# Stick-breaking attention: one scan and one product for both heads of a pair

## The chip, the cores and the metric

The kernel runs on one core of a Trainium2 chip. The metric is the device time of one execution in microseconds, the median of several runs. Times inside an execution come from the hardware profiler's trace of one execution. The engines are TensorE (PE in the profile, its weight loads PEld), VectorE (DVE), ScalarE (ACT), GpSimd (POOL) and SyncE (SP), on whose queue most DMAs are issued.

## The reference

The model is a trunk of two residual layers over 512 tokens of width 1024. Layer 0 mixes tokens with eight stick-breaking attention heads beside a state space model, layer 1 with sparse attention; each mixer is followed by an MLP, and a layer norm stands behind each of the four parts. The change is in the stick-breaking heads:

```python
z = jnp.einsum('bqhd,bshd->bhqs', q_b, k).astype(jnp.float32) * scale
causal = (spos[None, :] < tpos[:, None])[None, None]
log_beta = jax.nn.log_sigmoid(z)
log_1mb = jnp.where(causal, jax.nn.log_sigmoid(-z), 0.0)
csum = jnp.cumsum(log_1mb, axis=-1)
log_w = log_beta + csum[..., -1:] - csum
w = jnp.where(causal, jnp.exp(log_w), 0.0).astype(v.dtype)
return jnp.einsum('bhqs,bshd->bqhd', w, v)
```

The weight of key s is sigmoid(z_s) times the product of sigmoid(-z) over all later keys. There are 8 heads of 64 columns, and queries go in blocks of 128.

## The kernel before, in words

The kernel is one program for one core. It is written with a framework that tracks the tiles, puts a wait wherever two instructions share one, and plans the order of all engines' instructions when the program is built, by a model of their times; so an instruction need not stand in its queue where the source has it. Each engine then executes its own queue in order. A tile that is allocated with a tag takes turns among that tag's buffers, and a new user waits until the old one's readers are done. `tc.issue_after(x)` puts instructions behind x on the same engine.

`mixer_sb_ssm` (L666) is layer 0's mixer. It projects the input, runs the state space model in four groups, and projects q and k in four pairs of heads (`projections`, L763). Then a pool "att" is opened (L747), the norm's parameters are loaded (`gb`, L749, with the two DMAs of L168 and L169), and the attention of pairs 0, 1 and 2 follows, the gate of the state space model (`glu`, L776), pair 3, and the output projection in two halves (L760 and L761). The second half ends in the first layer norm, which reads `gb` at L185 and L189. The tag "gb" has one buffer; before `gb` it holds the phases `e` of the state space model (L514), which L616, L617, L627 and L628 read.

`stack_qk` (L880) splits a pair's q and k into a high and a low part (ScalarE at L889, GpSimd at L890) and moves them by DMA into `qst` and `kst`. `attention` (L901) does one pair: for each of four query blocks (`qb`), with nk = 128, 256, 384 or 512 keys, TensorE makes the logits of both heads in two PSUM banks (L914) and adds the causal mask (L918). Then, for each head in turn: ScalarE makes e = sigmoid(-z/8) (L922) and bt = sigmoid(z/8) (L923); VectorE scans e from the last key to the first with state = e * state + 0, starting from 1, into w (L925), reading the addend from one column of zeros with step 0; and it multiplies w by bt (L926). The e that the scan reads is shifted by one key, and GpSimd writes a 1 behind the last (L921). e has three buffers and bt two, each for one head; w has two, each for both heads. TensorE transposes the weights (`transpose_weights`, L934, L942), ScalarE copies them out of PSUM (L943), and TensorE multiplies by the values (L949). The marks of L931 place the first half of the output projection: its eight blocks stand behind nothing, nothing, nothing, and then the weighted values of query blocks 0, 0, 1, 1 and 2 of the last pair.

Of the kernel before, what the change touches and what calls it, by code (L numbers as in the profile page):

```python
# [8 lines left out]
F32 = mybir.dt.float32  # L9
F32R = mybir.dt.float32r  # L10
AF = mybir.ActivationFunctionType
ALU = mybir.AluOpType
# [3 lines left out]
P = 128  # L16
S = 512
D = 1024
KT = D // P
NB = S // P  # L20
# [15 lines left out]
class Trunk:  # L36
# [629 lines left out]
    def mixer_sb_ssm(self, w_in, w_out, w_glu, g, b):  # L666
        nc, a, tc = self.nc, self.a, self.tc
        act, vec, pool = nc.scalar, nc.vector, nc.gpsimd
        with tc.tile_pool(name="ps0", bufs=2, space=PSUM) as self.psb, \
# [76 lines left out]
            self.load_x()  # L746
            with tc.tile_pool(name="att", bufs=2, reuse_waits="tile") as ap:  # L747
                self.hlp = ap
                gb = self.ln_params(g, b)  # L749
                chi, clo = self.xhi, self.xlo  # L750
                rows = lambda kk, c0: self.w_rows(w_out, kk * 256, c0)
                att = lambda pr: self.attention(pr, self.stack_qk(qks[pr], ap), ap, v, msk_r)
                att(0)
                att(1)
                att(2)
                with tc.issue_after(self.last_move.ins):
                    self.fill_x()
                self.glu(w_glu, bgl, uTs, [t[:, i, :] for t in qks[:2] for i in range(2)], chi, clo)
                att(3)
                self.out_proj(chi, clo, rows, range(4, 8), True, None)  # L760
                self.out_proj(chi, clo, rows, range(4), False, gb)  # L761

    def projections(self, w_in, v, qks):  # L763

# [136 lines left out]
    def attention(self, pr, qk, ap, v, msk_r):  # L901

        nc = self.nc
        act, vec = nc.scalar, nc.vector
        qst, kst = qk
        self.kept = True
        cs = slice(pr * P, (pr + 1) * P)
        for qb in range(NB):
            nk = (qb + 1) * P
            qs = slice(qb * P, (qb + 1) * P)  # L910
            zs = [self.abank([P, 512], "psz") for _ in range(2)]
            for h in range(2):
                for part in range(2):
                    nc.tensor.matmul(zs[h][:, :nk], qst[:, h, qs], kst[:, h, part, :nk], start=part == 0, stop=False)  # L914
            w = ap.tile([P, 2, S], F32, tag="aw", name=self.nm("aw"))
            zero = self.zero.to_broadcast([P, nk])
            for h in range(2):
                nc.tensor.matmul(zs[h][:, nk - P:nk], self.ident_r, msk_r, start=False, stop=True)  # L918
                e = ap.tile([P, S + 1], F32, tag="ae", bufs=3, name=self.nm("ae"))
                bt = ap.tile([P, S], F32, tag="ab", bufs=2, name=self.nm("ab"))  # L920
                nc.gpsimd.memset(e[:, nk:nk + 1], 1.0)  # L921
                act.activation(e[:, :nk], zs[h][:, :nk], AF.Sigmoid, scale=-0.125)  # L922
                act.activation(bt[:, :nk], zs[h][:, :nk], AF.Sigmoid, scale=0.125)  # L923
                wv = w[:, h, :nk]
                vec.tensor_tensor_scan(wv[:, ::-1], e[:, 1:nk + 1][:, ::-1], zero, 1.0, ALU.mult, ALU.add)  # L925
                vec.tensor_tensor(wv, wv, bt[:, :nk], ALU.mult)  # L926
            wt = ap.tile([P, NB, 2, P], F32, tag="wt", name=self.nm("wt"))
            self.transpose_weights(w, wt, qb, nc.scalar.copy)
            if qb == 0:
                po = self.abank([P, S], "pso", True)  # L930
            self.marks[qb] = self.weighted_values(po[:, qs], wt, v, (cs.start, cs.start + 64), qb)  # L931
        self.split(self.xhi[:, pr, :], self.xlo[:, pr, :], po)
# [275 lines left out]
```

## Time and profile before

| | us |
|---|---|
| median of 3 runs | 1164.22 |
| the three runs | 1163.82, 1164.22, 1166.73 |
| the profiled execution | 1163.17 |
| its span, first to last instruction | 1161.4 |

In the profile, a line such as L925 is a line of the kernel, and `aw<-ae,two` names the tile that is written and those that are read: `ae` is e, `ab` is bt, `aw` is w, `wt` the transposed weights, `psz` the logits, `pst` the transposes in PSUM, `pso` the weighted values. In a timeline, a row gives the start, how long it took, the engine, the line, and how many instructions were merged into the row (the first one's shape is printed); in brackets stands how long the engine had been idle before it and who ended that. A matmul's recorded time holds its pipeline's latency too, so that rows of TensorE overlap.

### The profile page before, as it was taken

Reading aid. Unit: us, or ns where it says so; the run is one execution under the profiler, and the core shown is the slowest. Engines: PE = TensorE matmul, PEld = TensorE weight load, DVE = VectorE, ACT = ScalarE, POOL = GpSimd, SP = SyncE. Lnnn points to the kernel's source line nnn. Section 1 sums busy time; section 2 is a strip of 40 time slices with the busy share of each in tenths; the row PEclk is TensorE's granted clock in tenths of the full one; section 3 lists DMA queues with packets and bytes.
Section 4 is the critical chain, followed back from the end, with each engine's and each line's share of the span. In section 5 each row is a group of like instructions: output and inputs, shape, how many; then the busy total and the mean of one; then the engine's idle time right before and its main releaser. Section 6 shows DMA issues by size and latency. Waiting matters only on the chain.

```text
span 1161.4 us, 15563 instructions
## 1 busy us (share of the span) xinstructions
PE 1111.9 (96%) x5860; PEld 926.4 (80%) x5860; DVE 840.6 (72%) x1255; ACT 532.6 (46%) x832; POOL 172.2 (15%) x201
## 2 busy tenths in 40 slices
PE   7989999999999999999999979997999999999997
PEld 6878877779888888888898867775988888888886
DVE  7996598694667875965568998557548678587736
ACT  5534386424544444554135446552445445445520
POOL 1043230320000000000121655325000000000001
PEclk9998999999999999999999989998999999999999
DMA  7526683651243252333046860008304415315101
GB/s 246 143 62 157 189 223 96 194 168 39 61 145 101 62 159 73 97 112 87 1 120 158 216 189 1 2 9 264 109 19 127 131 33 152 120 38 162 37 1 73
DMA packets 147307, 126.99 MB, mean 109 GB/s; under 512 B 24353, under 2 KB 115297, under 8 KB 147233
## 3 DMA queue, kind: packets, MB, share of 16 engines
q1 hardware_dynamic: 145552, 123.59, 36.9%
q10 hardware_dynamic: 1680, 2.41, 0.6%
q8 instruction: 46, 0.75, 0.3%
q14 instruction: 29, 0.23, 0.1%
HBM read 105.80 MB, written 5.37 MB: 96 GB/s over the span
## 4 chain that ended last, share of the span: by engine, by line
PE 85%; DVE 6%; DMA 4%; issue 2%; ACT 2%; SPq 1%; POOL 0%; POOLq 0%; DVEq 0%; ACTq 0%
PE psa L131 12%; PE psa L133 12%; PE psa L132 12%; PE psb L311 7%; PE psb L313 7%; PE psb L312 7%; PE pso L949 3%; PE pst L942 3%; PE psb L382 3%; PE psb L381 3%; PE psb L380 3%; PE psl L1142 2%; PE psb L841 2%; PE psb L842 2%; PE psb L843 2%
## 5 line engine op out<-in xcount | busy, mean ns | idle before, releaser
L133 PE MATMUL psa<-xhi,wlo 128*128 128x512 f32 (+1 forms) x720 | 267.0, 371 | 0.0
L132 PE MATMUL psa<-xlo,whi 128*128 128x512 f32 (+1 forms) x720 | 266.5, 371 | 0.0
L131 PE MATMUL psa<-xhi,whi 128*128 128x512 f32 (+1 forms) x720 | 265.6, 371 | 0.2 <-ACT xhi L202 0.2
L104 ACT CAST whi<-raw 128x1024 fp32r<-128x1024 f32 (+1 forms) x129 | 133.6, 1046 | 204.6 <-PE psa L132 126.4
L105 DVE TENSOR_TENSOR wlo<-raw,whi 128x1024 fp32r<-128x1024 f32 (+1 forms) x102 | 128.2, 1260 | 86.9 <-ACT whi L104 85.8
L132 PEld LDWEIGHTS psa<-xlo,whi 128*128 128x128 f32 x720 | 135.7, 188 | 23.3 <-DVE xlo L203 0.4
L133 PEld LDWEIGHTS psa<-xhi,wlo 128*128 128x128 f32 x720 | 135.7, 188 | 23.2
L131 PEld LDWEIGHTS psa<-xhi,whi 128*128 128x128 f32 x720 | 135.0, 188 | 23.1 <-ACT xhi L202 0.5
L299 DVE TENSOR_TENSOR wlo<-b,whi 128x1024 fp32r<-128x1024 f32 x84 | 102.6, 1222 | 42.9 <-ACT whi L298 42.8
L311 PE MATMUL psb<-whi,whi 128*128 128x512 f32 x336 | 130.7, 389 | 0.0
L312 PE MATMUL psb<-wlo,whi 128*128 128x512 f32 x336 | 130.7, 389 | 0.0
L313 PE MATMUL psb<-whi,wlo 128*128 128x512 f32 x336 | 129.7, 389 | 0.0
L298 ACT CAST whi<-b 128x1024 fp32r<-128x1024 f32 x84 | 88.3, 1051 | 41.9 <-PE psb L313 30.2
L105 POOL TENSOR_TENSOR wlo<-raw,whi 128x1024 fp32r<-128x1024 f32 x27 | 69.7, 2591 | 135.6 <-ACT whi L104 134.5
L184 POOL TENSOR_TENSOR rs<-rs,two 128x1 f32<-128x1 f32 x16 | 22.4, 1402 | 424.2 <-DVE rs L183 424.2
L313 PEld LDWEIGHTS psb<-whi,wlo 128*128 128x128 f32 x336 | 63.1, 188 | 13.2
L312 PEld LDWEIGHTS psb<-wlo,whi 128*128 128x128 f32 x336 | 63.1, 188 | 13.1
L311 PEld LDWEIGHTS psb<-whi,whi 128*128 128x128 f32 x336 | 63.1, 188 | 13.0
L293 DVE TENSOR_TENSOR b<-b,b 128x1024 f32<-128x1024 f32 x48 | 60.3, 1262 | 12.3 <-DMA b<-in_w_dram 11.8
L298 ACT CAST whi<-h 128x1024 fp32r<-128x1024 f32 x36 | 38.0, 1054 | 54.0 <-PE psb L312 34.0
L299 DVE TENSOR_TENSOR wlo<-h,whi 128x1024 fp32r<-128x1024 f32 x36 | 44.0, 1222 | 14.2 <-ACT whi L298 13.5
L841 PE MATMUL psb<-whi,xhi 128*128 128x512 f32 x128 | 51.6, 411 | 0.8 <-DVE rs L183 0.6
(263 smaller groups left out, 1967.5 us busy)
## 6 DMA issues: line engine op xcount, KB each, us to landing
raw<-in_w_dram SPq DMA_DIRECT2D x80, 512.0 KB, 4.1
b<-in_w_dram SPq DMA_DIRECT2D x48, 512.0 KB, 4.6
raw<-in_w_in_dram SPq DMA_DIRECT2D x29, 512.0 KB, 4.4
raw<-in_w_out_dram SPq DMA_DIRECT2D x16, 512.0 KB, 4.6
qst<-hl SPq DMA_DIRECT2D x48, 128.0 KB, 3.5
kst<-hl SPq DMA_DIRECT2D x24, 256.0 KB, 4.4
gb<-in_ln_g_dram SPq DMA_DIRECT2D x4, 512.0 KB, 4.0
gb<-in_ln_b_dram SPq DMA_DIRECT2D x4, 512.0 KB, 5.2
```

Source lines behind the costliest of these rows:

```text
L104: nc.scalar.copy(hi[:, c], raw[:, c])
L105: (eng or nc.vector).tensor_tensor(lo[:, c], raw[:, c], hi[:, c].bitcast(F32), ALU.subtract)
L131: mm(ps, lhi, rhi, start=start, stop=False)
L132: mm(ps, lhi, rlo, start=False, stop=False)
L133: mm(ps, llo, rhi, start=False, stop=stop)
L293: vec.tensor_tensor(o, p, q, op)
L298: act.copy(hi, src)
L299: vec.tensor_tensor(lo, src, hi.bitcast(F32), ALU.subtract)
L311: mm(ps, lh, bhi[:, k, :], start=i + k == 0, stop=False)
L312: mm(ps, lh, blo[:, k, :], start=False, stop=False)
L313: mm(ps, ll, bhi[:, k, :], start=False, stop=i + k == 2)
L841: nc.tensor.matmul(ps, chi[:, k, tok], whi, start=i == 0, stop=False)
```

## The change

For each block of queries, e and bt become one tile each for both heads, with the two heads' columns one behind the other; there are two sets of them, for odd and for even blocks, each with one buffer. e has one column more than 2 x nk, and GpSimd writes zeros at columns nk and 2 nk, where a head begins when it is read backward. One scan over 2 x nk columns takes e as its factor and a row of zeros and ones as its addend: at the first column of each head the factor is 0 and the addend 1, so the state becomes 1, and everywhere else the addend is 0. Then one multiply does both heads. ScalarE no longer computes e for key 0, which the scan does not read.

The rows of zeros and ones for the four block lengths are overlapping windows of one strip of 1792 columns, filled by GpSimd before the attention. The strip lies in the tag "gb", where the norm's parameters lay; those are now loaded after the attention, at the call of the second half of the output projection. The tile w is read as one row of 2 x nk columns.

```diff
--- before.py
+++ after.py
@@ -746,7 +746,16 @@
             self.load_x()
             with tc.tile_pool(name="att", bufs=2, reuse_waits="tile") as ap:
                 self.hlp = ap
-                gb = self.ln_params(g, b)
+
+                ones = self.cp.tile([P, 2, D], F32, tag="gb", bufs=1, name="ones").rearrange("p r d -> p (r d)")
+                pool.memset(ones[:, 0:1792], 0.0)
+                self.ones, at = [None] * NB, 511
+                pool.memset(ones[:, at:at + 1], 1.0)
+                for qb in (3, 2, 1, 0):
+                    nk = (qb + 1) * P
+                    self.ones[qb] = ones[:, at - nk + 1:at + nk + 1]
+                    at += nk
+                    pool.memset(ones[:, at:at + 1], 1.0)
                 chi, clo = self.xhi, self.xlo
                 rows = lambda kk, c0: self.w_rows(w_out, kk * 256, c0)
                 att = lambda pr: self.attention(pr, self.stack_qk(qks[pr], ap), ap, v, msk_r)
@@ -758,7 +767,7 @@
                 self.glu(w_glu, bgl, uTs, [t[:, i, :] for t in qks[:2] for i in range(2)], chi, clo)
                 att(3)
                 self.out_proj(chi, clo, rows, range(4, 8), True, None)
-                self.out_proj(chi, clo, rows, range(4), False, gb)
+                self.out_proj(chi, clo, rows, range(4), False, self.ln_params(g, b))
 
     def projections(self, w_in, v, qks):
 
@@ -913,17 +922,20 @@
                 for part in range(2):
                     nc.tensor.matmul(zs[h][:, :nk], qst[:, h, qs], kst[:, h, part, :nk], start=part == 0, stop=False)
             w = ap.tile([P, 2, S], F32, tag="aw", name=self.nm("aw"))
-            zero = self.zero.to_broadcast([P, nk])
+
+            tag, n = (f"{qb % 2}", S if qb % 2 else 384)
+            e = ap.tile([P, 2 * n + 1], F32, tag="ae" + tag, bufs=1, name=self.nm("ae"))[:, :2 * nk + 1]
+            bt = ap.tile([P, 2 * n], F32, tag="ab" + tag, bufs=1, name=self.nm("ab"))[:, :2 * nk]
+            nc.gpsimd.memset(e[:, nk::nk], 0.0)
             for h in range(2):
                 nc.tensor.matmul(zs[h][:, nk - P:nk], self.ident_r, msk_r, start=False, stop=True)
-                e = ap.tile([P, S + 1], F32, tag="ae", bufs=3, name=self.nm("ae"))
-                bt = ap.tile([P, S], F32, tag="ab", bufs=2, name=self.nm("ab"))
-                nc.gpsimd.memset(e[:, nk:nk + 1], 1.0)
-                act.activation(e[:, :nk], zs[h][:, :nk], AF.Sigmoid, scale=-0.125)
-                act.activation(bt[:, :nk], zs[h][:, :nk], AF.Sigmoid, scale=0.125)
-                wv = w[:, h, :nk]
-                vec.tensor_tensor_scan(wv[:, ::-1], e[:, 1:nk + 1][:, ::-1], zero, 1.0, ALU.mult, ALU.add)
-                vec.tensor_tensor(wv, wv, bt[:, :nk], ALU.mult)
+                act.activation(e[:, h * nk + 1:h * nk + nk], zs[h][:, 1:nk], AF.Sigmoid, scale=-0.125)
+                act.activation(bt[:, h * nk:h * nk + nk], zs[h][:, :nk], AF.Sigmoid, scale=0.125)
+
+            wv = w.rearrange("p h k -> p (h k)")[:, :2 * nk]
+            vec.tensor_tensor_scan(wv[:, ::-1], e[:, 1:][:, ::-1], self.ones[qb][:, ::-1], 0.0, ALU.mult, ALU.add)
+            vec.tensor_tensor(wv, wv, bt, ALU.mult)
+            w = wv.rearrange("p (h k) -> p h k", k=nk)
             wt = ap.tile([P, NB, 2, P], F32, tag="wt", name=self.nm("wt"))
             self.transpose_weights(w, wt, qb, nc.scalar.copy)
             if qb == 0:
```

## Rows read from the trace of the kernel before

**Rows 1.** Page, section 1: busy us (share of the span) xinstructions.

```profile
PE 1111.9 (96%) x5860; PEld 926.4 (80%) x5860; DVE 840.6 (72%) x1255; ACT 532.6 (46%) x832; POOL 172.2 (15%) x201
```

**Rows 2.** Windows: length, busy us (xinstructions) by engine, granted clock, DMA share, GB/s.

```profile
148.00:184.00 36.00, 34.64 (x213) 27.27 (x215) 33.50 (x48) 27.79 (x61) 10.63 (x21) 1.00 0.77 219
184.00:196.00 12.00, 10.33 (x90) 7.77 (x85) 10.15 (x19) 10.00 (x26) 0.79 (x8) 0.95 0.24 58
196.00:209.00 13.00, 11.08 (x84) 8.41 (x85) 10.23 (x18) 8.71 (x22) 0.49 (x5) 0.91 0.00 1
209.00:219.00 10.00, 10.00 (x69) 7.86 (x67) 4.51 (x6) 3.18 (x4) 0.00 (x0) 1.00 0.53 155
219.00:236.00 17.00, 16.90 (x74) 13.35 (x72) 12.55 (x13) 6.51 (x7) 10.60 (x4) 1.00 1.05 308
```

**Rows 3.** DVE timeline, 187 to 210 us: start, us, instruction, [idle before].

```profile
189.83 1.81 DVE L925 TENSOR_TENSOR_SCAN aw<-ae,two 128x384 f32<-128x384 f32 x2
191.56 0.53 DVE L926 TENSOR_TENSOR aw<-aw,ab 128x384 f32<-128x384 f32 x1
192.01 1.22 DVE L925 TENSOR_TENSOR_SCAN aw<-ae,two 128x512 f32<-128x512 f32 x1
193.14 0.53 DVE L926 TENSOR_TENSOR aw<-aw,ab 128x384 f32<-128x384 f32 x1
...
196.24 0.67 DVE L926 TENSOR_TENSOR aw<-aw,ab 128x512 f32<-128x512 f32 x1
...
202.41 1.81 DVE L925 TENSOR_TENSOR_SCAN aw<-ae,two 128x384 f32<-128x384 f32 x2 [0.51 <-PE pst L942]
...
204.59 1.22 DVE L925 TENSOR_TENSOR_SCAN aw<-ae,two 128x512 f32<-128x512 f32 x1
205.72 0.53 DVE L926 TENSOR_TENSOR aw<-aw,ab 128x384 f32<-128x384 f32 x1
```

**Rows 4.** DVE timeline, 148 to 150 us: the first block.

```profile
148.42 0.42 DVE L925 TENSOR_TENSOR_SCAN aw<-ae,two 128x128 f32<-128x128 f32 x1 [0.40 <-issue]
148.95 0.29 DVE L926 TENSOR_TENSOR aw<-aw,ab 128x128 f32<-128x128 f32 x1
```

**Rows 5.** ACT timeline, 187 to 210 us: sigmoids of second heads, 512 keys.

```profile
191.69 0.67 ACT L922 ACTIVATE ae<-psz 128x512 f32<-128x512 f32 x1
...
204.10 0.67 ACT L922 ACTIVATE ae<-psz 128x512 f32<-128x512 f32 x1
```

**Rows 6.** PE timeline, 190 to 215 us: transposes that waited for a multiply.

```profile
193.73 0.66 PE L942 MATMUL pst<-ident,aw 128*128 128x128 f32 x4 [1.08 <-DVE aw L926]
...
206.31 0.66 PE L942 MATMUL pst<-ident,aw 128*128 128x128 f32 x4 [1.08 <-DVE aw L926]
```

**Rows 7.** Waits, 140 to 250 us: total us, times, longest us.

```profile
ACT ab L923 <- DVE aw L926: 7.9, 10, 2.4
...
DVE aw L925 <- PE pst L942: 4.6, 3, 2.2
```

**Rows 8.** Lines L925 and L926: count, duration ns min/median/max, first and last start.

```profile
L925 DVE TENSOR_TENSOR_SCAN aw<-ae,two x32: 409/932/1516, 148.4 to 206.8; 128x128 f32<-128x128 f32 x8, 128x256 f32<-128x256 f32 x8, 128x384 f32<-128x384 f32 x8, 128x512 f32<-128x512 f32 x8
...
L926 DVE TENSOR_TENSOR aw<-aw,ab x32: 260/478/1540, 148.9 to 208.5; 128x128 f32<-128x128 f32 x8, 128x256 f32<-128x256 f32 x8, 128x384 f32<-128x384 f32 x8, 128x512 f32<-128x512 f32 x8
```

**Rows 9.** SP queue timeline, 120 to 215 us.

```profile
123.78 0.35 SPq L168 DMA_DIRECT2D gb<-in_ln_g_dram  x1
...
181.00 3.22 SPq L851 DMA_DIRECT2D kst<-hl  x4
211.75 0.39 SPq L101 DMA_DIRECT2D raw<-in_w_out_dram  x1
```

**Rows 10.** Source line L700 and the POOL timeline, 95 to 250 us.

```profile
L700 POOL MEMSET tt<- x1: 955/955/955, 1.1 to 1.1; 128x1024 f32 x1
...
135.49 0.13 POOL L921 MEMSET ae<- 128x1 f32 x2 [15.10 <-PE py L646]
```

**Rows 11.** DVE timeline, 118 to 245 us: first use of the norm's parameters.

```profile
236.56 1.27 DVE L185 SCALAR_TENSOR_TENSOR x<-x,mv,gb 128x1024 f32<-128x1024 f32 x1
```

## The prediction

> **What bounds the kernel now.** I read the page's first section first: TensorE is busy 96% of the span [rows 1], so the attention's scans on VectorE matter only where TensorE waits for them. The windows by stage say where that is [rows 2]. From 148 to 184 us, the first two pairs, projections and the gate's matmuls fill TensorE: 34.64 of 36 us, 1.36 idle. [...] From 209 to 236 it is full again (10.00 of 10, 16.90 of 17). So whatever brings the attention's end forward in 184 to 209 is carried to the end of the kernel, at most 1.67 + 1.92 + 1.8 = 5.4 us, and nothing after 209 can be gained by faster scans.
>
> What ends TensorE's waits there is seen in the timeline of its matmuls: 1.08 us twice ahead of the transposes of a block's weights, each ended by the multiply of L926 [rows 6]. The DVE timeline shows why these multiplies are late [rows 3]: they belong to the block of 384 keys, whose two scans start at 189.83, but the second multiply stands behind the first scan of the 512-key block (192.01, 1.22 us) and ends only at 193.14 + 0.53 = 193.67. TensorE starts at 193.73. The same happens at 204.59 and 205.72, with TensorE starting at 206.31. The chain is: scan, a scan of the next block, multiply, transpose.
>
> **The DVE work that is removed.** Sixteen blocks (four pairs, four query blocks) had two scans and two multiplies; they get one of each over twice the columns, so 16 scans and 16 multiplies go. No column is saved. What an instruction costs beyond its columns has two prices. From starts [rows 3]: 512 columns of scan hold the engine 193.14 - 192.01 = 1.13 us, 384 columns (191.56 - 189.83) / 2 = 0.865, so 2.07 ns a column and 0.07 us an instruction; a multiply of 384 columns holds it 0.45 us (192.01 - 191.56), which at half the scan's price per column leaves 0.05. Sixteen times 0.12 is 1.9 us. From durations: the shortest scan is 0.409 us and the shortest multiply 0.260, both of 128 columns [rows 8], against 1.22 for 512 and 0.53 for 384 [rows 3]; that leaves 0.14 and 0.125 an instruction, together 16 x 0.265 = 4.2 us. I take 1.9, since consecutive starts are what the engine gives up, and keep 4.2 for the range.
>
> [...]
>
> **The DVE step that is added.** Two scans and then two multiplies mostly keep a multiply away from its own scan. One scan followed by its own multiply does not. The first block shows what that costs: the 128-column scan at 148.42 is followed by its multiply at 148.95 [rows 4], 0.53 us later, where 128 columns need 128 x 2.07 ns + 0.07 = 0.33. So 0.20 us a block, 3.2 us for sixteen if nothing else lies between, 0 if something does. VectorE's net is therefore between -4.2 and -1.9 + 3.2 = +1.3 us. In 184 to 209 little else is queued on it, so there I take eight blocks at 0.20 - 0.12 = +0.08, about +0.6 us of work; it is inside the starts worked out below. In the first two pairs I take nothing, since TensorE has other work.
>
> **The second operand of the scan.** A column of zeros read with step 0 becomes a full row of zeros and ones. No row shows a scan with two full rows. The multiplies read two full rows at about half the scan's time per column [rows 3], so the read keeps up: 0; the other bound is that it slows, which nothing in the trace suggests.
>
> **Where the gain goes.** With one instruction per block the multiply of the 384-key block can follow its scan. From 189.83: scan of 768 columns 768 x 2.07 ns + 0.07 = 1.66, the step 0.20, the multiply 768 x 1.04 ns + 0.13 = 0.93: done at 192.62 instead of 193.67, 1.05 us sooner. In the last pair, with scans from 202.41 and the multiply done at 206.25 [rows 3], it is the same 1.05. Then the 512-key block: its scan needs the sigmoids of both heads, and that of the second head runs 191.69 to 192.36 and 204.10 to 204.77 [rows 5]. The merged scan can start at 192.6, right after the multiply's columns, so this new wait costs nothing: 2.2 + 0.2 + 1.2 gives 196.2, against 196.24 + 0.67 = 196.9 now [rows 3]. What is late next is TensorE itself. Sum: 2 x 1.05 = 2.1 us.
>
> **ScalarE and the buffers.** Now e has three one-head buffers and bt two; then there are two sets of both heads. ScalarE waited 7.9 us in ten places for a multiply to free bt [rows 7]; blocks two apart now share, so most of that goes. It was no end of the chain: the scans that idled waited for TensorE's transposes to free the weights' tile (4.6 us, three times [rows 7]), and that tile keeps its two buffers. I take 0; the bound is that part of the 4.6 goes too. The first column of e is no longer computed: 0.
>
> **GpSimd.** 32 small memsets become 16; they wait for scans and nobody waits for them beyond what now shows. Added is a fill of 1792 columns with five single ones: 1024 columns took 0.955 us [rows 10], so 1.7 us and some 0.5. It can start once the phases' tile is free, about 123.7 (the DMA into that same tile went at 123.78 [rows 9]); GpSimd sits idle for 15.1 us up to 135.49 [rows 10], which hides it. Without that cover it would delay the splits of the first pair's q and k by 2.2 us.
>
> **The norm's parameters.** Two DMAs of 0.5 MB leave 123.78 on SP's queue, and come after the last scan, about 208. Their queue has nothing between 181 and the load at 211.75 [rows 9]; the fabric moves 1 GB/s from 196 to 209 [rows 2]. First use is at 236.56 [rows 11], so some 28 us of slack. Queued behind them are the last output weight and the MLP's weights; 1 MB at 308 GB/s [rows 2] is 3.4 us, the most that they could come late, in a stretch where TensorE has its operands. I take 0. Should they stand ahead of the loads of 160 to 171 us, these would wait for the last scan; that the queue held loads in the order of their readiness speaks against it.
>
> **How this stands to the runs.** The profiled execution took 1163.17 us, 1.05 below the median of 1164.22. 1163.17 - 2.1 = 1161.1 in its terms, 1162.1 against the median.
>
> **The rivals.** (a) No net change: the dependent step eats what the merge returns and TensorE finds another wait, the transposes of the block before being the next. That gives 1164.2. For it: VectorE's net is near zero, and the order of all engines is planned anew, which can move TensorE's small groups either way. (b) VectorE's busy time, 53.9 of 61 us from 148 to 209 [rows 2], sets the pace, and an instruction returns its whole duration price: 4.2 us, 1160.0; with all of TensorE's idling and the lower clock gone, 1158.8. [...] Against it: the starts. (c) Slower: the merged scan of the 512-key block stands ahead of the multiply of the 384-key block, as one of its halves does today. Then that multiply ends at 189.83 + 1.66 + 2.2 + 0.93 = 194.6, 0.95 later than now; at four pairs 3.8 us, 1168.0, with another stretch of low clock like today's 1.8 us up to 1169.8. It decides by whether the second head's sigmoid is ready when the scan before ends: today it is 0.5 to 0.7 us later (192.36 against 191.64, 204.77 against 204.22; [rows 3, 5]), but the larger buffers let ScalarE run ahead.
>
> **How the numbers follow.** Forecast 1162.1 with a chance of 0.42, its own range 1160.2 to 1163.6; (a) 0.20; (b) 0.16; (c) 0.22, of which half lies above 1167.7. The range 1158.8 to 1167.5 leaves out about half of (c) and little else. What measurement can tell here is 0.3%, 3.5 us: below 1160.7 lie most of (b) and a part of the forecast, 0.27; above 1167.7 half of (c) and some that none of these names, 0.17; the rest, 0.56, is no change.
>
> **What would show it.** The two waits of 1.08 us ahead of the transposes are gone or moved; each multiply follows its scan by some 0.2 us more than columns; the scans of 1024 columns take 2.2 to 2.3 us (more would mean that the full operand slows them); the granted clock of the last two pairs is at least as high; the parameters' DMAs stand near 208 and the first norm starts no later than now. It is wrong if multiplies stand behind merged scans, if the weights' transposes leave longer gaps, or if TensorE idles at 219 to 252 for weights.

## The result: slower by 0.8%, and the profile after

The changed kernel took 1173.38 us in the median (1171.00 to 1176.07), the kernel before, in the same runs, 1164.02 (1163.64 to 1166.73). The ratio is 1.0080, with a 95% interval of 1.0063 to 1.0098: 9.3 us slower, where 1162.1 was forecast and 1167.5 was the end of the range. (Ratios, here and below, are not quotients of the medians and can differ a little from them.) The profiled execution after took 1171.00 us (span 1169.2), that of before 1163.17 (span 1161.4), so the two traces show 7.8 of these 9.3 us.

First the page's busy line of the kernel after, which answers to [rows 1], and its windows, which answer to [rows 2]; 236 to 252 us is added.

```profile
PE 1113.5 (95%) x5860; PEld 929.5 (80%) x5860; DVE 838.2 (72%) x1223; ACT 531.7 (45%) x832; POOL 173.1 (15%) x191
...
148.00:184.00 36.00, 30.11 (x187) 24.48 (x187) 32.31 (x31) 29.38 (x66) 10.64 (x13) 0.91 0.81 230
184.00:196.00 12.00, 9.68 (x87) 7.63 (x85) 9.67 (x10) 8.96 (x24) 0.51 (x5) 1.00 0.07 18
196.00:209.00 13.00, 8.68 (x69) 6.61 (x69) 9.23 (x9) 7.42 (x18) 0.10 (x1) 0.89 0.13 52
209.00:219.00 10.00, 10.00 (x65) 7.50 (x64) 1.76 (x3) 4.08 (x7) 1.69 (x1) 0.97 0.69 198
219.00:236.00 17.00, 17.00 (x77) 14.08 (x76) 11.53 (x12) 4.00 (x4) 8.44 (x4) 1.00 1.00 338
236.00:252.00 16.00, 16.00 (x76) 13.12 (x74) 12.96 (x20) 2.30 (x3) 3.06 (x2) 1.00 0.24 68
```

VectorE has 32 instructions fewer and its busy time falls from 840.6 to 838.2 us. TensorE's work is the same, and it is what got worse. As an estimate, busy time times granted clock, it does from 148 to 209 us 30.11 x 0.91 + 9.68 + 8.68 x 0.89 = 44.8 us of full-clock work, where before it did 34.64 + 10.33 x 0.95 + 11.08 x 0.91 = 54.5. Some 4 us of these 9.7 come back later by the same estimate: from 236 to 252 it is full now (16.00 of 16, clock 1.00), where before it was busy for 13.38 us at a clock of 0.89. The rest stays: the fourth norm of layer 0's mixer begins at 266.75 us, before at 259.85.

TensorE's waits after, from its timeline (start, us, instruction, [idle before <- what ended it]); before there were the two of 1.08 us in [rows 6], with one of 0.51 and one of 0.84 ahead of them:

```profile
171.34 0.62 PE L923 MATMUL psz<-kst,qst 128*128 128x384 f32 x2 [2.87 <-ACT ab L933]
...
180.20 0.63 PE L954 MATMUL pst<-ident,aw 128*128 128x128 f32 x4 [2.18 <-DVE aw L937]
...
192.10 0.85 PE L954 MATMUL pst<-ident,aw 128*128 128x128 f32 x6 [0.91 <-DVE aw L937]
194.79 0.88 PE L961 MATMUL pso<-wt,v 128*64 128x128 f32 x12 [1.08 <-DVE xlo L864]
...
206.22 1.51 PE L954 MATMUL pst<-ident,aw 128*128 128x128 f32 x6 [3.87 <-DVE aw L937]
```

VectorE's timeline after, around the last of these waits, and the first output block:

```profile
201.28 3.94 DVE L936 TENSOR_TENSOR_SCAN aw<-ae,ones 128x768 f32<-128x768 f32 x2 [0.51 <-PE pst L954]
205.13 0.94 DVE L937 TENSOR_TENSOR aw<-aw,ab 128x768 f32<-128x768 f32 x1
205.98 0.69 DVE L864 TENSOR_TENSOR xlo<-pso,xhi 128x512 fp32r<-128x512 f32 x1
206.58 1.22 DVE L937 TENSOR_TENSOR aw<-aw,ab 128x1024 f32<-128x1024 f32 x1
215.05 0.69 DVE L855 SCALAR_TENSOR_TENSOR x<-x,psb 128x512 f32<-128x512 f32 x1 [7.25 <-PE psb L852]
```

The scans of 768 and 1024 columns stand one behind the other (x2 at 201.28, 3.94 us), and the product that TensorE waits for comes behind both. That is the mechanism of rival (c). The line at 215.05 shows something that no part of the prediction had: it is the first of the eight blocks of the output projection's first half. In the kernel before, three of these blocks were done some 36 us earlier, while TensorE would have waited for the attention; the waits of 2.87 and 2.18 us above lie where they are missing. VectorE's timeline of before, where L846 is the same line of code:

```profile
178.63 0.69 DVE L846 SCALAR_TENSOR_TENSOR x<-x,psb 128x512 f32<-128x512 f32 x1
...
179.70 0.69 DVE L846 SCALAR_TENSOR_TENSOR x<-x,psb 128x512 f32<-128x512 f32 x1
...
184.98 0.67 DVE L846 SCALAR_TENSOR_TENSOR x<-x,psb 128x512 f32<-128x512 f32 x1
```

### The profile page after: what moved, and what is told of

Same layout as the page of the kernel before. It is cut to its first block, busy times and chain, and to the rows that moved or that the text cites. A ratio compares the mean times of both kernels' runs of the same rounds, so it can differ in the third digit from the quotient of the medians.

```text
span 1169.2 us, 15481 instructions
## 1 busy us (share of the span) xinstructions
PE 1113.5 (95%) x5860; PEld 929.5 (80%) x5860; DVE 838.2 (72%) x1223; ACT 531.7 (45%) x832; POOL 173.1 (15%) x191
## 4 chain that ended last, share of the span: by engine, by line
PE 86%; DVE 6%; DMA 4%; issue 1%; ACT 1%; SPq 1%; POOL 0%; POOLq 0%; DVEq 0%; ACTq 0%
PE psa L131 12%; PE psa L132 12%; PE psa L133 12%; PE psb L311 7%; PE psb L313 7%; PE psb L312 7%; PE pso L961 3%; PE pst L954 3%; PE psb L382 2%; PE psb L381 2%; PE psb L380 2%; PE psb L850 2%; PE psb L852 2%; PE psb L851 2%; PE psl L1154 2%
## 5 line engine op out<-in xcount | busy, mean ns | idle before, releaser
L320 DVE TENSOR_TENSOR x<-x,psb 128x512 f32<-128x512 f32 x80 | 51.4, 679 | 0.1
```

The source lines that it names most:

```text
L320: vec.tensor_tensor(xs, xs, ps, op)
```

## The experiments

Each ran beside the kernel before on the same chip; not all experiments ran on one chip, so two of them are best compared by their ratios, which carry 95% intervals. One fact of the code is needed for the first ones. `bank()` takes a PSUM bank from one of two pools, "psb" or "psc" (two buffers, and the attention's transposes use it), by the parity of a counter, and `nm()` advances the same counter each time that it makes a name. `ln_params` makes one name. Moved from ahead of the attention to behind the first half of the output projection, it no longer counts for these eight blocks. Before, all eight take psb; after, all eight take psc.

**The moved loads alone.** Before, with the loads late and two added counts that keep every bank.

```diff
-                gb = self.ln_params(g, b)
+                self.n += 1
 ...
-                self.out_proj(chi, clo, rows, range(4), False, gb)
+                self.n += 1
+                self.out_proj(chi, clo, rows, range(4), False, self.ln_params(g, b))
```

> The kernel before, with only the load of the norm's parameters moved to the second half of the output projection, and the counter held so that all blocks keep their pools. Theory C, the late DMAs: 1168 to 1173. Theories A and B: 1162 to 1166; the two DMAs go out when their tile is free, as before, since nothing lies in it in this kernel, so this run tests only the new place in the program, not the wait for the last scan.

1163.94 us, ratio 0.9996 [0.9986, 1.0005]. The place of the call costs nothing. The DMAs themselves are not late here: in this kernel nothing else lies in their tile, and they go out at 124.45 and 124.84 us. That late DMAs cost nothing rests on the trace of the kernel after (shown under what held).

**The bank alone.** Before, with only the parity of the first half shifted.

```diff
+                self.n += 1
                 self.out_proj(chi, clo, rows, range(4, 8), True, None)
+                self.n += 1
                 self.out_proj(chi, clo, rows, range(4), False, gb)
```

> The kernel before, with only the counter of names moved on by one ahead of the first half of the output projection (and back behind it), so that its eight blocks take banks of psc. Nothing else is changed. Theory A, the pool: 1169 to 1175, the first of the eight blocks behind the last pair, TensorE idle some 4 us more between 148 and 184. Theories B and C: 1164, as before.

1169.36 us, ratio 1.0041 [1.0027, 1.0055]: 4.8 us from a name's number, as expected if the pool matters. Its window of the first pairs, and its first output block on VectorE:

```profile
148.00:184.00 36.00, 31.56 (x200) 24.56 (x201) 34.85 (x49) 29.96 (x67) 11.09 (x22) 0.91 0.81 225
...
211.53 0.69 DVE L848 SCALAR_TENSOR_TENSOR x<-x,psb 128x512 f32<-128x512 f32 x1 [5.17 <-PE psb L845]
```

TensorE is busy for 31.56 us at 0.91 instead of 34.64 at 1.00, and the first block comes at 211.53, not at 178.63: the blocks that filled TensorE's gaps are gone from there.

**The bank put back in the changed kernel.** Two added counts give the eight blocks psb again.

```diff
+                self.n += 1
                 self.out_proj(chi, clo, rows, range(4, 8), True, None)
+                self.n += 1
                 self.out_proj(chi, clo, rows, range(4), False, self.ln_params(g, b))
```

> The changed kernel, with the counter of names moved on by one ahead of the first half of the output projection and once behind it. The method bank() chooses the PSUM pool by whether that counter is odd; the change has moved the norm's parameters, whose tile takes one number, behind these eight blocks, and so moved all eight from the pool psb to psc, which the transposes of the attention use. Theory A, the pool: the three free blocks stand beside the attention again, ahead of 186 us, and the time comes back by about 8 us, to 1162 to 1166. Theory B, the merged scan itself (a scan that waits for three sigmoids, a multiply that waits for the whole scan): it stays at 1170 to 1176. Theory C, the late DMAs of the norm's parameters: it stays at 1170 to 1176 too.

1170.95 us, ratio 1.0055 [1.0039, 1.0072]: 2.4 us nearer to before by the medians, 2.9 by the ratios, whose intervals overlap. That is less than the 4.8 that the bank cost alone and far from the 1162 to 1166 that were expected if the pool carried the whole loss. Three blocks are early again (the first at 180.67), and what is late next is rival (c), now in both of the last pairs. VectorE and TensorE in the last pair:

```profile
206.12 3.93 DVE L938 TENSOR_TENSOR_SCAN aw<-ae,ones 128x768 f32<-128x768 f32 x2
209.96 2.07 DVE L939 TENSOR_TENSOR aw<-aw,ab 128x768 f32<-128x768 f32 x2
...
211.04 1.51 PE L956 MATMUL pst<-ident,aw 128*128 128x128 f32 x6 [4.07 <-DVE aw L939]
```

**The order on VectorE.** Each merged scan is put behind the product of the block before it, in the kernel with the banks put back.

```diff
+            with self.tc.issue_after(self.last_mul) if self.last_mul else nullcontext():
                 vec.tensor_tensor_scan(wv[:, ::-1], e[:, 1:][:, ::-1], self.ones[qb][:, ::-1], 0.0, ALU.mult, ALU.add)
-            vec.tensor_tensor(wv, wv, bt, ALU.mult)
+            self.last_mul = vec.tensor_tensor(wv, wv, bt, ALU.mult).ins
```

> after_psb, and on VectorE each merged scan is put behind the multiply of the block before it, so that no scan of 1024 columns stands ahead of the multiply of 768. In after_psb that happened in the last two pairs, and TensorE waited 2.65 and 4.07 us ahead of the transposes. Theory D, that order: 1164 to 1167, and these two waits at 1.1 us or less. Theory E, the merge in itself (a scan that waits for the sigmoids of both heads, transposes that wait for both heads' multiply): it stays at 1169 to 1172, with the wait moved elsewhere.

1168.28 us, ratio 1.0028 [1.0012, 1.0043], some 3 us better than without the order by the ratios, whose intervals just overlap. TensorE's waits for a product fall from 2.65 and 4.07 us to 0.68 and 1.90, but two new ones of 1.09 and 1.85 us appear, for the split of the pair's output into xhi and xlo, which stands behind the merged scan of 1024 columns. The later of each:

```profile
204.77 0.84 PE L958 MATMUL pst<-ident,aw 128*128 128x128 f32 x6 [1.90 <-DVE aw L941]
207.47 1.55 PE L965 MATMUL pso<-wt,v 128*64 128x128 f32 x12 [1.85 <-DVE xlo L867]
```

The same order on the kernel after as it is, with the blocks in psc:

> The changed kernel with the same order on VectorE, its eight blocks still in psc. Theory D, with the pool as a cost of its own: 1168 to 1171, some 3 us below the changed kernel and some 4 above after_psb_order. If the pool alone carries the loss: 1172 to 1175.

1177.94 us, ratio 1.0111 [1.0086, 1.0136]: a miss. It was expected to help there too, and the kernel became 4.5 us slower by the medians (the intervals of the two ratios overlap). The blocks stay late, and part of the loss lies at 830 us, in code that no edit touched (below, the run that moves a cast). This kernel and the one before it, run on the same chip, differ in the bank alone: 9.7 us.

The corresponding order on the kernel before (a block's first scan behind both products of the block before):

```diff
+                with self.tc.issue_after(self.last_mul) if self.last_mul and not h else nullcontext():
                     vec.tensor_tensor_scan(wv[:, ::-1], e[:, 1:nk + 1][:, ::-1], zero, 1.0, ALU.mult, ALU.add)
-                vec.tensor_tensor(wv, wv, bt[:, :nk], ALU.mult)
+                mul = vec.tensor_tensor(wv, wv, bt[:, :nk], ALU.mult).ins
+            self.last_mul = mul
```

> The kernel before, and on VectorE the first scan of a block is put behind both multiplies of the block before. Theory D: the two waits of 1.08 us ahead of the transposes go, 1161 to 1163.5. If the place of the multiply does not set the end: 1163.5 to 1165.

1163.87 us, ratio 0.9989 [0.9977, 1.0002]: no gain that can be told from none, though both waits of 1.08 us in [rows 6] are gone. In their place TensorE waits 0.83 us for a copy of ScalarE and 0.95 us for the output split, which stands behind a 512-key scan:

```profile
205.25 1.52 PE L952 MATMUL pso<-wt,v 128*64 128x128 f32 x12 [0.95 <-DVE xlo L856]
```

The next layer norm, behind the first MLP, begins at 566.49 us, in the kernel before at 566.53. (This trace is of the slowest of its ten executions, 1167.04 us; it falls behind only later, in layer 1.)

**The tiles without the merge.** The kernel with the banks put back, its tiles and its addend strip, but one scan and one product per head.

```diff
+            for h in range(2):
+                c = slice(h * nk, h * nk + nk)
+                vec.tensor_tensor_scan(wv[:, c][:, ::-1], e[:, 1:][:, c][:, ::-1], self.ones[qb][:, c][:, ::-1], 0.0,
+                                       ALU.mult, ALU.add)
+                vec.tensor_tensor(wv[:, c], wv[:, c], bt[:, c], ALU.mult)
```

> after_psb with its tiles (two sets for both heads, zeros and ones as addend), but one scan and one multiply for each head, as before the change. Theories D and E: 1162 to 1166, since both lay the rest on the merge. If the tiles, the addend row or the late parameters behind the last scan are at fault: 1168 or more.

1172.78 us, ratio 1.0068 [1.0042, 1.0094], as slow as the merged one; a miss for every theory that blamed the merged instructions. Both scans of 512 columns stand ahead of the second product of 384 here as well (2.33 us, at 198.42 and 212.16). So the order is not a matter of merged instructions but of the plan, and something else of the change moves the plan.

**The addend strip alone.** Every version with the changed tiles put the last gelu's steps ahead of the splits for the gate on VectorE, at 143 to 148 us; no version of before did. Of the parts of the change, put one by one into the kernel before, the fill of the addend strip turned the planned order in the same way; more buffers, tiles for both heads or the missing first column did not (these three are planned orders, not runs). So: the run of the moved loads, plus that fill, which nothing reads.

```diff
+                ones = self.cp.tile([P, 2, D], F32, tag="gb", bufs=1, name="ones").rearrange("p r d -> p (r d)")
+                pool.memset(ones[:, 0:1792], 0.0)
```

> Before, with the norm's parameters loaded late, the banks held as in before, and one added instruction: the fill of the 1792-column strip on GpSimd, which nothing reads. Attention is untouched (one scan and one product per head). Theory E (the plan at the start): the fill alone makes the plan put the last gelu block's steps ahead of the splits for the gate's product on ScalarE and VectorE, so that the first scan comes some 16 us after the convolution's last matmul instead of 13.4, with a stretch at half clock behind it: 1166 to 1168 us. Rival T (the later start comes from the merged scan and its tiles): the start is as in before, 13.2 to 13.6 us, and the time 1163.5 to 1165.

1167.60 us, ratio 1.0019 [1.0007, 1.0032]; without the fill it was 0.9996. An instruction that GpSimd executes in an idle stretch, and that no instruction of the attention waits for, makes the kernel 2 to 3 us slower, and the order of the other engines is another one. It also holds back the parameters' DMAs, which go out at 128.61 us instead of 124.45, but the next run has a loss of this size without that. (The fill isn't the only trigger: in the changed kernel the planned order stays turned when the fill is written elsewhere; no run shows that.) The windows 148 to 153 us of before and of this kernel, each with VectorE ahead of it:

```profile
148.00:153.00 5.00, 4.62 (x27) 3.95 (x27) 4.16 (x7) 3.95 (x12) 2.81 (x4) 1.00 0.97 296
...
144.06 1.28 DVE L783 SCALAR_TENSOR_TENSOR xlo<-uT,xhi 128x512 fp32r<-128x512 f32 x2
```

```profile
148.00:153.00 5.00, 4.85 (x17) 4.16 (x18) 4.01 (x7) 4.46 (x11) 2.94 (x4) 0.66 0.84 254
...
145.10 0.43 DVE L661 TENSOR_SCALAR gt<-gt 128x512 f32<-128x512 f32 x1 [0.69 <-ACT gt L660]
145.56 0.69 DVE L662 TENSOR_TENSOR gt<-gt,y 128x512 f32<-128x512 f32 x1
146.17 1.89 DVE L787 SCALAR_TENSOR_TENSOR xlo<-uT,xhi 128x512 fp32r<-128x512 f32 x3
```

The gate's splits (xlo, x3) come at 146.17 behind two gelu steps; before, two of them came at 144.06. TensorE idles 1.51 us, and 1.57 up to 148.15, and its granted clock is 0.66 over these 5 us; before, it idled 1.35 and 1.08 and the clock was 1.00.

**That order alone.** Before, with the gate's three splits put behind the two gelu steps, and no other order given.

```diff
+            with self.tc.issue_after(self.last_gelu):
                 vec.scalar_tensor_tensor(glo[:, q, :], ge[q], 0.5, ghi[:, q, :].bitcast(F32), ALU.mult, ALU.subtract)
```

> Before, with only VectorE's three splits for the gate's product ordered behind the two VectorE steps of the last gelu block; ScalarE's order stays that of before. Theory E with VectorE's order as the cause: 1165.5 to 1167.5 us and a first scan 15 us or more after the convolution's last matmul. Theory E with ScalarE's order as the cause (tanh, a copy and a cast stand ahead of the sigmoids' table load there): 1164 to 1165, first scan at 13.2 to 14.2 us.

1168.75 us, ratio 1.0035 [1.0021, 1.0050], more than expected: 4 us for two short instructions in front of three. ScalarE's order there is that of before; TensorE's own was planned anew with VectorE's. TensorE's timeline:

```profile
146.73 0.41 PE L915 MATMUL psz<-kst,qst 128*128 128x128 f32 x2 [2.25 <-issue]
...
149.15 0.49 PE L915 MATMUL psz<-kst,qst 128*128 128x128 f32 x2 [1.90 <-DMA qst<-hl]
```

It idles 2.25 and 1.90 us, and the clock is 0.66 from 148 to 153.

**The start put right in the merged kernel.** The kernel with banks and order, with the splits of three blocks written ahead of the last gelu and its first VectorE step behind the second of them.

```diff
+                for q in range(3):
+                    act.activation(ghi[:, q, :], uTs[q], AF.Copy, scale=0.5)
+                    self.last_split = vec.scalar_tensor_tensor(glo[:, q, :], uTs[q], 0.5, ghi[:, q, :].bitcast(F32),
+                                                               ALU.mult, ALU.subtract).ins
+                    if q == 1:
+                        gelu(3, ys[3])
 ...
+        with self.tc.issue_after(self.last_split) if self.last_split else nullcontext():
             vec.tensor_scalar(t, t, 0.044715, 1.0, ALU.mult, ALU.add)
```

> The changed kernel with the banks as before, each merged scan behind the multiply before it, and the gate's splits of three blocks written ahead of the last gelu, so that VectorE's order at the start is that of before (two splits, a gelu step, a split, a gelu step) and tanh no longer stands ahead of the first sigmoid. Theory E: the start is some 2.5 us earlier than with banks and order alone (first scan 13.2 to 14.5 us after the convolution's last matmul), and the time falls from 1168.3 to 1165 to 1166.5: near before, no longer clearly slower. Theory T (merged scan and its tiles cost by themselves): 1167.5 to 1169.

1166.19 us, ratio 1.0015 [1.0002, 1.0028], inside the expected band; but the first scan still came 15.8 us after the convolution's last matmul, and the clock fell all the same (0.50 from 148 to 153). The measure was a bad one: a merged first scan needs the sigmoids of both heads, and before, the second head's scan did not start sooner (150.87). With ScalarE's order put back too:

```diff
+        with self.tc.issue_after(self.last_hi) if self.last_split else nullcontext():
             act.activation(t, y, AF.Square)
```

> As the run that held the start, with ScalarE's order at the start put back too: the last gelu block's square stands behind two of the gate's copies, as in before (in that run it still stood ahead of all of them, and TensorE idled 1.60 and 0.68 us there with half clock behind it from 147.4). Theory E (the rest of the loss is still the start): TensorE stays at full clock over 148 to 153 as in before, and the time is 1163.5 to 1165.2. Theory M (the rest is the merged pair itself: its scan of 1024 columns, 2.28 us, holds the output split and the multiply longer than the scan of 512 did): no change, 1165.7 to 1166.7.

1166.95 us, ratio 1.0029 [1.0018, 1.0039]: no further gain, and a miss for the theory of the start. TensorE's granted clock was not 1.00 there but 0.66 (148 to 153), so the run does not say what a start at full clock is worth.

**The output split in front.** As the last one, with a pair's scan of 1024 columns behind the output split of the pair before.

```diff
+            held = self.last_out if pr and qb == 3 else self.last_mul
+            with self.tc.issue_after(held) if held else nullcontext():
 ...
+        self.last_out = vec.tensor_tensor(self.xlo[:, pr, :], po, self.xhi[:, pr, :].bitcast(F32), ALU.subtract).ins
```

> As the run with both orders at the start, and the scan of 1024 columns in a pair put behind the output split of the pair before it, which stood behind it so far (TensorE's second product waited 1.08 and 1.85 us for that split). Theory M: these two waits go, the multiply of that block comes 0.6 us later in cover, and the time is 1 to 2.5 us below the run without this order. Theory E: within 0.7 us of it.

1166.87 us, ratio 1.0033 [1.0020, 1.0046]: no change in time, which spoke for the theory of the start. The profile says otherwise. TensorE's two waits for the split are gone, and the fourth norm begins at 258.01 us, 7.4 earlier than in the run before it (the clock from 148 to 153 is 1.00 here, 0.66 there: some 1.7 of the 7.4 by an estimate, 5 x 0.34) and 1.8 earlier than in the kernel before. The gain is lost again 560 us later, in layer 1. TensorE and ScalarE there, in this kernel, and ScalarE in the kernel before:

```profile
819.93 0.74 PE L133 MATMUL psa<-xhi,whi 128*128 128x256 f32 x4 [1.90 <-ACT xhi L204]
821.90 0.58 PE L134 MATMUL psa<-xlo,whi 128*128 128x256 f32 x1 [1.23 <-DVE xlo L205]
...
818.35 1.04 ACT L106 CAST whi<-raw 128x1024 fp32r<-128x1024 f32 x1 [2.88 <-DMA raw<-in_w_dram]
819.30 2.04 ACT L204 CAST xhi<-pst 128x512 fp32r<-128x512 f32 x4
```

```profile
817.89 1.08 ACT L202 CAST xhi<-pst 128x512 fp32r<-128x512 f32 x2 [0.74 <-PE pst L199]
819.92 1.05 ACT L104 CAST whi<-raw 128x1024 fp32r<-128x1024 f32 x1 [0.96 <-DMA raw<-in_w_dram]
820.88 1.06 ACT L202 CAST xhi<-pst 128x512 fp32r<-128x512 f32 x2
```

Four copies of transposed blocks (xhi, x4) stand behind a weight cast that waits 2.88 us for its DMA. Before, two of them stand ahead of that cast. TensorE idles 0.33 us for a sum into x, 1.90 for the copies and 1.23 for a split, and its granted clock is 0.91 from 820 to 840 us, before 1.00.

**That cast alone.** The same kernel, with the one cast put behind the two copies.

```diff
-            nc.scalar.copy(hi[:, c], raw[:, c])
+            with self.tc.issue_after(self.hold) if self.hold else nullcontext():
+                nc.scalar.copy(hi[:, c], raw[:, c])
 ...
+                        self.hold = self.turned[1] if first and f == 7 and self.n_mlp == 2 else None
                         ps = self.proj_fm(w1, (c * 8 + f) * P, None)
```

> As the run with the output split in front, and one cast of the second feed-forward layer's weights put behind the four transposed blocks' copies on ScalarE that it stood behind in the kernel before (in that run it stands ahead of them and waits 2.88 us for its DMA at 818, so that TensorE idles 0.33, 1.90 and 1.23 us there and falls to half clock). Theory P (the plan shifts in code that the change does not touch, and this one place holds what is left): the time falls from 1166.9 by 3 to 4.5 us to 1162.3 to 1164, level with before or a little under it. Rival M (the merged pair's own work holds the rest): within 1 us of 1166.9.

1162.12 us, ratio 0.9978 [0.9969, 0.9987]: from the place of one cast 4.8 us by the medians, 6.4 by the ratios. TensorE has no wait any more from 813 to 830 us, and the merged kernel is now faster than the kernel before, by 2.6 us. This loss belongs to the plan of the kernel with the orders added: the changed kernel itself has no such waits there, and TensorE is busy for all of 820 to 840 us at a clock of 0.99.

The profiled execution of this kernel was the slowest of its eleven, 1165.48 us. From 148 to 153 us, in the kernel with the output split in front and in this one, which has the same order there:

```profile
148.00:153.00 5.00, 5.00 (x31) 4.43 (x30) 2.04 (x4) 4.77 (x13) 2.50 (x3) 1.00 0.94 302
```

```profile
148.00:153.00 5.00, 5.00 (x15) 4.15 (x16) 2.00 (x4) 4.45 (x11) 2.45 (x3) 0.50 0.97 301
```

TensorE had idled 1.43 and 0.86 us ahead in the first, 1.83 and 0.91 in the second. The second runs at a granted clock of 0.50, and its next norm behind the first MLP begins 2.7 us later (567.34 against 564.67). So a clock read from one trace need not belong to the order, here or in the runs above.

**The order without the merge.** Is that gain the merge's? The kernel before, one scan and one product per head, with both scans of a 512-key block behind the output split.

```diff
+                with self.tc.issue_after(self.last_out) if pr and qb == 3 else nullcontext():
                     vec.tensor_tensor_scan(wv[:, ::-1], e[:, 1:nk + 1][:, ::-1], zero, 1.0, ALU.mult, ALU.add)
 ...
+        self.last_out = vec.tensor_tensor(self.xlo[:, pr, :], po, self.xhi[:, pr, :].bitcast(F32), ALU.subtract).ins
```

> Before, still one scan and one product per head, with one order added on VectorE: both scans of a pair's 512-key block stand behind the output split of the pair before it, as in the merged kernel that came out 0.2% under before. If that gain belongs to this order, 1161.5 to 1163 us; if it belongs to the merged instructions (fewer starts, shorter dependent steps), 1163.5 to 1165.

1159.67 us, ratio 0.9962 [0.9950, 0.9973]: the fastest kernel of all, without any merge, and below both expected bands. The order alone gives 4.4 us by the ratio. TensorE's windows of the last pairs, and its waits there:

```profile
184.00:196.00 12.00, 11.49 (x108) 9.05 (x109) 10.29 (x19) 9.93 (x26) 0.79 (x8) 1.00 0.31 72
196.00:209.00 13.00, 11.87 (x89) 9.31 (x86) 12.36 (x22) 10.42 (x23) 0.59 (x6) 1.00 0.01 1
...
192.92 1.03 PE L944 MATMUL pst<-ident,aw 128*128 128x128 f32 x6 [0.51 <-DVE aw L927]
...
197.14 0.41 PE L944 MATMUL pst<-ident,aw 128*128 128x128 f32 x2 [0.73 <-DVE aw L927]
...
203.02 1.14 PE L944 MATMUL pst<-ident,aw 128*128 128x128 f32 x6 [0.32 <-DVE aw L927]
```

The waits are 0.51, 0.73 and 0.32 us; the two of 1.08 us in [rows 6] are gone and the clock is 1.00. This is what the prediction expected of the merge: each 384-key product now follows its scan, because the 512-key scan no longer stands between (the order holds it back behind the split). In the merged kernel with the cast moved, the waits of the same stretch are 0.68, 0.65 and 1.72, the last of them:

```profile
206.33 0.84 PE L973 MATMUL pst<-ident,aw 128*128 128x128 f32 x6 [1.72 <-ACT wt L974]
```

There the transposes come 3.32 us after the scan of 768 columns starts (203.01 us), with the separate instructions 2.40 us after the scans of 384 start (200.62 us), ahead of the end of the second head's product (203.35 us).

## Why the prediction was wrong, step by step

**The norm's parameters, "I take 0".** This is the step whose failure the runs price highest. The DMAs did cost nothing: in the trace after, they are issued at 205.25 us and no instruction waits for them. But the step counted what the moved call issues and not what it does while the program is built. It takes a number from the counter that chooses PSUM banks. In the kernel before that alone costs 4.8 us, in the changed kernel 2.4 to 2.9, with the order on VectorE 9.7, and it undoes work that the prediction took as given, the 34.64 busy microseconds of [rows 2]: "in the first two pairs I take nothing, since TensorE has other work". After the change it had less other work there (30.11 busy us).

**"GpSimd sits idle ... which hides it."** The fill took 1.61 us at 123.90, in the idle stretch, as worked out, and no instruction of the attention waited for it. Still, added to the kernel before, it costs 2 to 3 us, because this kernel's order is planned at build from modelled times, and one more instruction gives another plan. The first rival (a) did say that the order of all engines is planned anew and can move either way; its time, no net change, took the sum of such moves as zero. They were not: the start (2 to 4 us in the runs of the strip and of the gelu's order) and, in the kernel with the orders added, the cast at 818 us (4.8 or more) are each as large as the whole forecast gain. These prices do not add up to the 9.3 us: each was measured in another kernel, and each edit plans the rest anew.

**Rival (c).** Its mechanism came, in the last pair after, and in two pairs with the banks put back. Its working was exact for VectorE: scan of 768, scan of 1024, product are priced at 1.66 + 2.2 + 0.93 = 4.79 us, and took 201.28 to 206.07, 4.79. What it mis-sized is TensorE's loss. It took the product's lateness, 0.95 us. The wait grew from 0.84 and 1.08 us for the two heads [rows 6 has the second] to 3.87 for both at once, 1.95 more, because the first head's transposes can no longer start ahead of the second head's product. That coarser grain is a price of the merge that no step named. The order took some 3 us off the kernel with banks put back, against up to 3.8 in the working of (c).

**The order of the 384-key product.** The forecast's own step, two waits of 1.08 us gone for 2.1 us, assumed that one instruction per block puts the product behind its own scan; in the last pair the plan put the scan of 1024 columns between them instead. An order on VectorE does it without the merge, but ending the two waits is not enough: behind both products they go and nothing is gained (0.9989), and only with the output split ahead of the 512-key scans as well is the gain 4.4 us (the last run). Merged, with the banks, four orders and the cast put right, the gain is 2.6 us. That its median, 1162.12, is the forecast's time is luck. The separate version of the same order is nominally 1.9 us faster by the ratios, with intervals that overlap narrowly (0.9969 to 0.9973). Traces show what separates it from the merged kernel with the output split in front: TensorE lacks 1.64 us from 184 to 209, against 3.25 merged, and its clock from 236 to 252 is 1.00, against 0.89, some 1.8 us by an estimate (16 x 0.11); the next norm behind the first MLP begins at 561.65 us, against 564.67. The first is the coarser grain again; whether the clock belongs to the merge these traces don't show. So the merge itself gained nothing that these runs show. Since these two kernels also differ in their plans elsewhere, its own cost isn't measured cleanly; that stays open.

**The bound of 5.4 us.** Its first two terms are TensorE's idle time from 184 to 209 in [rows 2]. The third, 1.8 us for the lower clock, is shown by no run; it is the author's estimate from the granted clocks there, 0.95 and 0.91 (12 x 0.05 + 13 x 0.09). What the runs show in its place: in the trace before, matmuls of 512 columns start every 0.23 us at a granted clock of 1.00 (240 to 242 us) and every 0.43 us at 0.50 (247 to 249 us); and with the separate order the clock is 1.00 from 184 to 209, TensorE lacks 1.64 us there, and the whole gain is 4.4 us.

**What held.** The scan with a full addend row is not slower (2.28 us for 1024 columns, twice 1.22 for 512 before), the dependent step is 0.19 us, and the late loads and the fill themselves hide. VectorE, SyncE and GpSimd after:

```profile
162.75 2.28 DVE L936 TENSOR_TENSOR_SCAN aw<-ae,ones 128x1024 f32<-128x1024 f32 x1
165.13 1.23 DVE L937 TENSOR_TENSOR aw<-aw,ab 128x1024 f32<-128x1024 f32 x1
...
244.97 1.27 DVE L185 SCALAR_TENSOR_TENSOR x<-x,mv,gb 128x1024 f32<-128x1024 f32 x1
...
205.25 0.33 SPq L168 DMA_DIRECT2D gb<-in_ln_g_dram  x1
205.62 0.43 SPq L169 DMA_DIRECT2D gb<-in_ln_b_dram  x1
...
123.90 1.61 POOL L751 MEMSET ones<- 128x1792 f32 x1 [3.47 <-DVE sk L628]
```

1024 columns take 2.28 us, and their product starts 2.38 after the scan's start, where 1024 x 2.07 ns + 0.07 makes 2.19: 0.19 for the dependent step. The first norm starts at 244.97, long after its parameters' loads. VectorE's busy time, which doesn't count the dependent steps' gaps (here 0.10 us, from 165.03 to 165.13), fell by 840.6 - 838.2 = 2.4 us, between the 1.9 and the 4.2 of the two prices.

## What to carry to other kernels

Where a program's order is planned at build, and buffers are chosen by a counter, an edit has a price that none of its instructions shows: compare the planned order and the buffers' choice of both versions before costing durations, and hold them equal (a dummy count, an explicit order) to see what the edit itself does. Merging two heads' instructions took 2.4 us off VectorE's busy time here but made its consumer wait for both heads (3.87 us, where it had waited 0.84 and 1.08); an explicit order gave 4.4 us with the separate instructions, and 2.6 with the merged ones, once the banks, the start and a cast were put right as well. When a profile shows a stage ending earlier and the time does not follow, look for the place behind it where the gain is given back; here it lay 560 us behind.

## What the runs showed of the hardware that was not expected

Behind a short idling of TensorE the granted clock was lower in four of the six kernels below, and in two it was not; that the idling brings the lower clock is the author's reading, which no run shows by itself. At about 148 us TensorE idled twice; from 148 to 153 its granted clock was 1.00 after 1.35 and 1.08 us (the kernel before) and after 1.43 and 0.86 (output split in front), but 0.66 after 1.51 and 1.57 (the strip), 0.66 after 2.25 and 1.90 (the gelu's order), 0.50 after 1.60 and 0.68 (the start put right) and 0.50 after 1.83 and 0.91 (the cast moved). In the run of the gelu's order the idling grew by 1.72 us, and 5 us at 0.66 are worth another 1.7 by an estimate (5 x 0.34); together that is most of its 4 us. At 818 us the three idle stretches make 3.46, and 20 us at 0.91 another 1.8 by the same kind of estimate, where moving the cast gave 4.8 us by the medians.
